# The first query's projection takes its PSUM bank from the retention's pool instead of the shared projection pool

## The chip, the cores and the metric

The kernel runs on one core of a Trainium2 chip. The metric is the device time of one execution, in microseconds. Engines are named as in the profile: PE (TensorE, matrix multiplies), PEld (its weight loads), DVE (VectorE), ACT (ScalarE), POOL (GpSimd) and SP (SyncE, which only issues DMAs here).

## The reference

Two layers of a hybrid transformer on one sequence of 512 tokens, model width 1024, followed by a final norm. Each layer computes

```
h      = rms_norm(x)
proj   = h @ w_in                       # retention | DSA | dilated columns
mixed  = concat(retention_mixer, dsa_mixer, dilated_mixer)
x      = x + mixed @ w_out
x      = x + square(relu(rms_norm(x) @ w_up)) @ w_down
```

The retention mixer has 4 heads. The DSA mixer has 4 heads which attend to 128 selected keys per query (an indexer scores all keys, and a top-k picks them). The dilated mixer has 8 heads with three window patterns, which the kernel folds into one mask. All heads are 64 wide.

## The kernel before

Everything is kept in fp32 and multiplied as a high and a low part, so each projection of 128 columns (`wform`) is 8 blocks x 3 products = 24 matmuls of 128x512 into one PSUM bank. PSUM has 8 banks, in three pools: `mm` with two banks (all projections), `at` with four (scores, transposes, attention outputs), `rt` with two. The `rt` pool serves the four retention tiles of a layer (`ret_tile`), tokens 2 and 3 of the dilated values (`dil_v`: tokens 0 and 1 take `mm`, tokens 2 and 3 take `rt_bank()`) and a part of the MLP's down projection.

The attention part of a layer is emitted in this order: stage `tv` (token columns), `idx` (the indexer), `top` (the first round of the top-k), `dv0` (first half of the dilated values); then the projections of the first head pair, `q_of(heads[0], ...)` and `k_of(heads[0], ...)` (called q0 and k0 below); then a loop over 12 heads, in which `head_s` issues the scores and the softmax of a head, and the list `FILL` (`'q1,q2 k1 k2,g0,d g1,k3,...'`) adds the next projections: q1 beside head 0, then q2, k1 and k2, and so on. The `topk` rounds (16 per layer, each three MAX8 and three match-and-replace steps on DVE, lines 603 and 604) are spread over the same loop.

A projection that has ended in its bank is taken out of it in two halves of 64 partitions. `evac_q` (lines 424 and 425) does for each half an ACT activation and then a DVE operation which subtracts what ACT has written. `evac_k` (lines 437 to 439) does the same with a copy, a DMA of the high part and a DVE subtraction. The bank is free for the next projection when the second DVE operation has ended.

The Tile framework orders the instructions of each engine when the program is built: by their place in the code, shifted by the hand-set numbers in `PR`, and by its own model of when operands, buffers and banks come free. At run time each engine works through its queue in that fixed order. A bank is given to a tile by the same planner, out of those free in its pool at that point of the plan.

Weights come by DMA into `raw`, are split by ACT (line 278) and POOL or DVE (line 286) into one of 5 `w` buffers, and `done()` prepares the next unit after a projection has used one.

Of the kernel before, what the change touches and what calls it, by code (L numbers as in the profile page):

```python
# [123 lines left out]
class Kern:  # L124
# [665 lines left out]
        return self.evac_k(ps)  # L790

    def proj(self, key, act, cols=P):
        ps = self.mm()
        self.wform(self.unit(key), act, cols, ps, cols)
        self.done()
        return ps
# [336 lines left out]
```

## Time and profile before

| | |
|---|---|
| Median of 3 runs | 1234.67 us (1234.22 to 1235.9) |
| The profiled execution, device time | 1234.49 us |
| Its span, first to last instruction | 1232.7 us |
| PE busy | 1209.2 us, 98% of the span |
| DVE busy | 922.2 us, 75% |
| ACT busy | 678.8 us, 55% |
| POOL busy | 476.2 us, 39% |

The profiled execution lies 0.18 us below the median of the runs, and its time is 1.8 us above its own span. Busy times are sums over the whole program, which has stages with different limits: attention and MLP of layer 0, then the same for layer 1, whose first projection starts at 622 us.

### The profile page before, as it was taken

Reading aid. Unit: us, or ns where it says so; the run is one execution under the profiler, and the core shown is the slowest. Engines: PE = TensorE matmul, PEld = TensorE weight load, DVE = VectorE, ACT = ScalarE, POOL = GpSimd, SP = SyncE. Lnnn points to the kernel's source line nnn. Section 1 sums busy time; section 2 is a strip of 40 time slices with the busy share of each in tenths; the row PEclk is TensorE's granted clock in tenths of the full one; section 3 lists DMA queues with packets and bytes.
Section 4 is the critical chain, followed back from the end, with each engine's and each line's share of the span. In section 5 each row is a group of like instructions: output and inputs, shape, how many; then the busy total and the mean of one; then the engine's idle time right before and its main releaser. Section 6 shows DMA issues by size and latency. Waiting matters only on the chain. (4 is left out here: it accounts for less than half of the span.)

```text
span 1232.7 us, 16897 instructions
## 1 busy us (share of the span) xinstructions
PE 1209.2 (98%) x6116; PEld 1028.4 (83%) x6116; DVE 922.2 (75%) x1582; ACT 678.8 (55%) x1241; POOL 476.2 (39%) x461
## 2 busy tenths in 40 slices
PE   8999999999999999999999999999999999999997
PEld 6988888889888888888889888888798888888886
DVE  5599858776875967858857997687769668587596
ACT  6645658745544545545556456686455355354454
POOL 4443747553402304114223546764544032140232
PEclk9999999999999999999999999999999999999999
DMA  7432314216244071260153323241180622604201
GB/s 217 120 94 65 103 56 124 82 52 210 64 145 129 2 220 52 74 179 16 46 163 95 95 79 93 86 120 52 52 257 1 208 65 69 180 26 142 81 1 69
DMA packets 142180, 122.73 MB, mean 100 GB/s; under 512 B 6801, under 2 KB 114065, under 8 KB 142098
## 3 DMA queue, kind: packets, MB, share of 16 engines
q1 hardware_dynamic: 139600, 117.46, 31.9%
q10 hardware_dynamic: 2498, 4.20, 1.3%
q8 instruction: 48, 0.79, 0.3%
q14 instruction: 34, 0.28, 0.1%
HBM read 114.31 MB, written 4.19 MB: 96 GB/s over the span
## 5 line engine op out<-in xcount | busy, mean ns | idle before, releaser
L336 PE MATMUL mm<-act,w 128*128 128x512 f32 (+2 forms) x2352 | 516.1, 377 | 3.1 <-DVE Q L425 3.1
L336 PEld LDWEIGHTS mm<-act,w 128*128 128x128 f32 x2352 | 424.4, 188 | 79.8 <-issue 3.9
L286 POOL TENSOR_TENSOR w<-raw,w 128x512 fp32r<-128x512 f32 (+1 forms) x124 | 160.5, 1318 | 98.0 <-ACT w L278 73.0
L278 ACT CAST w<-raw 128x1024 fp32r<-128x1024 f32 (+1 forms) x138 | 143.1, 1038 | 77.3 <-PE rt L1039 27.6
L1039 PE MATMUL rt<-w,U 128*128 128x512 f32 x768 | 183.2, 389 | 0.0
L286 DVE TENSOR_TENSOR w<-rd,w 128x1024 fp32r<-128x1024 f32 x112 | 144.8, 1305 | 49.9 <-ACT w L278 49.9
L286 DVE TENSOR_TENSOR w<-raw,w 128x1024 fp32r<-128x1024 f32 (+1 forms) x76 | 93.8, 1235 | 102.0 <-ACT w L278 101.8
L1039 PEld LDWEIGHTS rt<-w,U 128*128 128x128 f32 x768 | 144.2, 188 | 29.9
L996 POOL TENSOR_TENSOR st<-s 128x256 f32<-128x256 f32 x32 | 39.1, 1222 | 330.1 <-ACT s L985 325.2
L278 ACT CAST w<-rd 128x1024 fp32r<-128x1024 f32 x112 | 117.5, 1049 | 83.4 <-PE rt L1039 41.7
L348 PE MATMUL mm<-w,act 128*128 128x456 f32 (+2 forms) x576 | 119.4, 353 | 2.2 <-DVE KL L439 1.2
L348 PEld LDWEIGHTS mm<-w,act 128*128 128x128 f32 x576 | 96.8, 190 | 15.3 <-DVE act L401 1.6
L348 PE MATMUL mm<-w,mix 128*128 128x512 f32 x384 | 98.3, 404 | 0.6 <-DVE Q L425 0.5
L1039 PE MATMUL at<-w,U 128*128 128x512 f32 (+1 forms) x396 | 97.7, 386 | 0.0
L304 DVE TENSOR_TENSOR rd<-rd,rd 128x1024 f32<-128x1024 f32 x64 | 94.3, 1473 | 0.6
L1039 PEld LDWEIGHTS at<-w,U 128*128 128x128 f32 x396 | 73.6, 188 | 15.0
L348 PEld LDWEIGHTS mm<-w,mix 128*128 128x128 f32 x384 | 71.2, 192 | 15.3 <-DVE Q L425 0.9
L983 ACT ACTIVATE s<-mm 128x512 f32<-128x512 f32 x62 | 36.9, 595 | 85.2 <-PE mm L336 75.6
L1000 ACT CAST U<-st 128x1024 fp32r<-128x1024 f32 x32 | 33.8, 1055 | 81.0 <-POOL st L997 81.0
L994 POOL TENSOR_TENSOR st<-s,s 128x256 f32<-128x256 f32 x32 | 36.7, 1146 | 92.0 <-ACT s L985 92.0
L464 ACT ACTIVATE ph<-ph,sm 128x128 f32<-128x128 f32 (+1 forms) x96 | 53.9, 563 | 24.6 <-DVE sm L463 23.6
L1001 DVE TENSOR_TENSOR U<-s,U 128x256 fp32r<-128x256 f32 x64 | 63.9, 999 | 0.0
(169 smaller groups left out, 1770.8 us busy)
## 6 DMA issues: line engine op xcount, KB each, us to landing
raw<-in_w_up_dram SPq DMA_DIRECT2D x64, 512.0 KB, 4.3
rd<-in_w_down_dram SPq DMA_DIRECT2D x32, 1024.0 KB, 5.1
raw<-in_w_in_dram SPq DMA_DIRECT2D x48, 512.0 KB, 3.9
raw<-in_w_out_dram SPq DMA_DIRECT2D x16, 512.0 KB, 4.1
xv<-in_x_dram SPq DMA_DIRECT2D x7, 512.0 KB, 4.8
KH<-KH ACTq DMA_DIRECT2D x24, 128.0 KB, 2.3
raw<-in_w_in_dram SPq DMA_DIRECT2D x8, 256.0 KB, 2.9
xd<-xv SPq DMA_DIRECT2D x4, 512.0 KB, 2.8
```

The source lines that it names most:

```text
L278: self.nc.scalar.copy(hi, src)
L286: eng.tensor_tensor(lo[:, i:i + step], src[:, i:i + step], hi[:, i:i + step].bitcast(F32), op=ALU.subtract)
L304: sub = lambda o, a, b: self.nc.vector.tensor_tensor(o, a, b, op=ALU.subtract)
L336: self.nc.tensor.matmul(ps[:cols, toks[0]:toks[1]], a, b, start=(k == 0 and j == 0), stop=(k == KB - 1 and j == 2))
L348: self.nc.tensor.matmul(ps[:, :w], a, b, start=(n == 0), stop=(n == tot - 1))
L464: nc.scalar.activation(p, p, AF.Exp, bias=a, scale=-1.0, accum_out=b)
L983: nc.scalar.activation(s, ps, AF.Relu)
L994: tt(st[:, 0], a[:, 1], d[:, 1], op=ALU.add)
L996: tt(st[:, 2], a[:, 0], a[:, 1], op=ALU.subtract)
L1000: nc.scalar.copy(hi, src)
L1001: nc.vector.tensor_tensor(lo, src, hi.bitcast(F32), op=ALU.subtract)
L1039: nc.tensor.matmul(ps[:, c0:c1], a, w, start=(new and n == 0), stop=(n == 11), skip_group_check=True)
```

## The change

`proj` makes the bank of a projection and is called by `q_of`, `k_of` and `gate`. For the key whose second and third items are `"dq"` and `0` (the dilated query projection of head pair 0, once in each layer), the tile now comes from `rt_bank()`; all other projections still call `mm()`. The number and form of the instructions are the same; the bank of q0, and what follows from it in the planner's order, is what can differ.

```
     def proj(self, key, act, cols=P):
-        ps = self.mm()
+
+        ps = self.rt_bank() if key[1:3] == ("dq", 0) else self.mm()
         self.wform(self.unit(key), act, cols, ps, cols)
         self.done()
         return ps
```

## Rows read from the trace of the kernel before

**Rows 1.** The cores view: span and mean granted TensorE clock.
```profile
core 0: 1232.7 us, clock 0.995
```

**Rows 2.** The page, part 1: busy us, share of the span, instructions.
```profile
PE 1209.2 (98%) x6116; PEld 1028.4 (83%) x6116; DVE 922.2 (75%) x1582; ACT 678.8 (55%) x1241; POOL 476.2 (39%) x461
```

**Rows 3.** Waits of PE, whole program: who waited for whom, total us, times, longest.
```profile
PE mm L336 <- DVE Q L425: 3.1, 2, 1.6
PE mm L348 <- DVE KL L439: 1.2, 2, 0.6
```

**Rows 4.** Timeline of layer 0, 72 to 92 us: start, us, engine, line, operation.
```profile
72.67 11.07 PE L336 MATMUL mm<-act,w 128*128 128x512 f32 x48
72.69 0.39 ACT L525 CAST xv<-rt 128x256 fp32r<-128x256 f32 x1
...
77.19 1.47 DVE L603 MAX8 top<-sc 128x8 f32<-128x384 f32 x3
78.34 0.59 ACT L424 ACTIVATE Q<-mm 64x512 fp32r<-64x512 f32 x1 [3.76 <-PE mm L336]
...
80.15 1.47 DVE L603 MAX8 top<-sc 128x8 f32<-128x384 f32 x3
81.65 0.68 DVE L425 SCALAR_TENSOR_TENSOR Q<-mm,Q 64x512 fp32r<-64x512 f32 x1
82.37 0.59 ACT L424 ACTIVATE Q<-mm 64x512 fp32r<-64x512 f32 x1 [2.50 <-DVE Q L425]
...
84.48 0.69 DVE L425 SCALAR_TENSOR_TENSOR Q<-mm,Q 64x512 fp32r<-64x512 f32 x1
...
85.32 5.73 PE L336 MATMUL mm<-act,w 128*128 128x512 f32 x24 [1.58 <-DVE Q L425]
85.45 0.53 ACTq L438 DMA_DIRECT2D KH<-KH  x1
...
88.30 0.69 DVE L439 TENSOR_TENSOR KL<-mm,KH 64x512 fp32r<-64x512 f32 x1
...
90.88 0.22 PE L444 MATMUL at<-KH,Q 128*128 128x128 f32 x1
...
91.12 0.70 DVE L439 TENSOR_TENSOR KL<-mm,KH 64x512 fp32r<-64x512 f32 x1
```

**Rows 5.** Timeline of PE in layer 0, after those rows.
```profile
92.16 4.72 PE L336 MATMUL mm<-act,w 128*128 128x512 f32 x20
...
97.30 0.40 PE L348 MATMUL rt<-w,act 128*128 128x256 f32 x2
...
127.37 3.10 PE L348 MATMUL mm<-w,act 128*128 128x256 f32 x24 [0.60 <-DVE KL L439]
```

**Rows 6.** Timeline of DVE in layer 0 just before 127.37 us.
```profile
126.53 0.69 DVE L439 TENSOR_TENSOR KL<-mm,KH 64x512 fp32r<-64x512 f32 x1
```

**Rows 7.** Busy time by stretch: length, then PE, PEld, DVE, ACT, POOL busy (instructions), clock, DMA.
```profile
72.67:127.37 54.70, 52.29 (x272) 44.00 (x270) 53.94 (x162) 29.48 (x60) 24.85 (x26) 1.00 0.33 84
...
142.00:190.00 48.00, 47.69 (x255) 40.36 (x253) 26.94 (x79) 29.77 (x66) 28.59 (x32) 1.00 0.28 81
679.88:734.55 54.67, 52.29 (x271) 44.00 (x270) 53.91 (x162) 29.47 (x60) 24.85 (x26) 1.00 0.32 84
```

**Rows 8.** DVE groups from 72.67 to 127.3 us: count, busy us, mean ns.
```profile
L604 DVE MATCH_REPLACE8 sc<-top,sc 128x512 f32<-128x512 f32 (+2 forms) x36 | 19.6, 550 | 0.1
L603 DVE MAX8 top<-sc 128x8 f32<-128x384 f32 (+2 forms) x36 | 18.6, 546 | 0.1
```

**Rows 9.** Timeline of layer 1, the same place as rows 4.
```profile
692.51 5.69 PE L336 MATMUL mm<-act,w 128*128 128x512 f32 x24 [1.56 <-DVE Q L425]
...
698.32 0.69 DVE L439 TENSOR_TENSOR KL<-mm,KH 64x512 fp32r<-64x512 f32 x1
...
699.31 4.76 PE L336 MATMUL mm<-act,w 128*128 128x512 f32 x20
```

**Rows 10.** The page, part 6: DMA of the key's high part, us to landing.
```profile
KH<-KH ACTq DMA_DIRECT2D x24, 128.0 KB, 2.3
```

More of the change, by code (lines that the diff above doesn't have):

```diff
@@ L792, in proj @@
     def proj(self, key, act, cols=P):
-        ps = self.mm()
+        ps = self.rt_bank() if key[1:3] == ("dq", 0) else self.mm()
         self.wform(self.unit(key), act, cols, ps, cols)
```

## The prediction

> **What bounds the kernel now.** I read the cores view first: one core, span 1232.7 us, TensorE at a mean granted clock of 0.995 [rows 1], which is the upper of its two levels (2.4 GHz) nearly throughout; nothing here hangs on the clock. The page's first part comes next: TensorE is busy for 98% of the span, VectorE for 75% [rows 2]. So over the whole program TensorE is the bound, and time can be won only where TensorE idles, or by less work for it; the change takes no work away.
>
> The third view is therefore TensorE's waits. The reader is to see one entry: TensorE's projections (line 336) wait for VectorE's line 425 twice, 3.1 us together, the longest 1.6 [rows 3]. This is the largest wait inside the layers, and 0.25% of the time. The timeline shows what it is. In layer 0 the 48 matmuls of q0 and k0 run from 72.67 to 83.74, into the two `mm` banks. The next projection, q1, needs one of these banks. That of q0 is free when the second half of `evac_q` ends on VectorE, at 84.48 + 0.69 = 85.17, and q1 starts 0.15 us later, at 85.32, after 1.58 us of idleness [rows 4]. Layer 1 does the same, with 1.56 us [rows 9].
>
> The change aims at exactly this wait. Whether it pays depends on the view read last, the busy time by stretch. From 72.67 to 127.37 us VectorE is busy for 53.94 of 54.70 us, and in layer 1 for 53.91 of 54.67 [rows 7]. The remainder, 0.76 us in each, is spread over 162 instructions. In this stretch it is VectorE that has no slack, whatever the 75% of the page say: 36 MAX8 and 36 match-and-replace steps of the top-k, 18.6 + 19.6 us, are queued between the evacuations [rows 8]. The first evacuation shows how late it runs: ACT ends the first half of q0 at 78.34 + 0.59 = 78.93, and VectorE's part starts at 81.65, behind rank work, 2.72 us later [rows 4].
>
> **The change part by part.** *The wait for q0's bank goes.* With q0 in a retention bank, k0 and q1 have the two `mm` banks, and q1 can start when k0 ends, at 83.74 instead of 85.32: 1.58 us in layer 0 and 1.56 in layer 1, 3.14 together [rows 4, 9].
>
> *What is late next.* q1 takes 90.88 - 85.32 = 5.56 us up to the scores of head 0, and these take 92.16 - 90.88 = 1.28 us [rows 4, 5]. Moved up, q1 ends at 89.30 and the scores at 90.58. The scores' own operands allow that: the first half of k0's low part is ready at 88.30 + 0.69 = 88.99, and the DMA issued at 85.45 lands some 2.3 us later, about 87.8 [rows 4, 10]. Behind the scores stands q2, and it needs an `mm` bank too. Of these, q1's has only just been filled; k0's is free when VectorE has done k0's second half, at 91.12 + 0.70 = 91.82 [rows 4]. With the 0.15 us seen above q2 starts at 91.97. It starts at 92.16 now [rows 5]. So of the 1.58 us, 0.19 remain, and TensorE waits 91.97 - 90.58 = 1.39 us at q2 instead, for line 439 instead of 425. In layer 1 the same bank is free at 698.32 + 0.69 = 699.01, q2 could start at 699.16, and starts at 699.31 now: 0.15 remain [rows 9]. Queued behind q2 on TensorE is everything else of the layer, since its queue is in order; no other matmul can fill the 1.39 us unless the planner has put one there.
>
> *And after that.* The 0.19 and 0.15 us do not reach the end either. At 127.37 TensorE waits again for VectorE, 0.60 us, for the low part that ends at 126.53 + 0.69 = 127.22 [rows 5, 6]. VectorE comes to this point through 54.55 us of nearly unbroken work, and none of this work becomes shorter or starts earlier by an earlier matmul. As long as VectorE's queue keeps its order, TensorE is at 127.37 when it was before. The remainder goes there, and the term of this part is 0 (bounds from this part: 0 to -0.34 us).
>
> *The retention bank as such.* The two `rt` banks hold tokens 2 and 3 of the dilated values until ACT has read them, for the first at 72.69 + 0.39 = 73.08, which is 0.41 us after q0's start of before [rows 4]. Either the planner lets k0 begin and switches to q0 when its bank is free, and TensorE loses nothing; or TensorE stands until 73.08 + 0.15 = 73.23, 0.56 us. Then k0 ends at 84.30, q1 at 89.86 and the scores at 91.14, still ahead of 91.97: the late bank is hidden by the wait at q2, and its term is 0. Without that cover it costs 2 x 0.56 = 1.12 us. At its other end the bank is held until 85.17, and the next matmuls into an `rt` bank start at 97.30 [rows 4, 5]: 12 us of room, term 0.
>
> *What follows q1's earlier end on other queues.* The number of instructions and DMAs is unchanged. ACT's evacuation of q1 and the split of the weights that take q1's buffer can come some 1.6 us earlier; ACT is busy for 29.48 of 54.70 us here and POOL for 24.85 [rows 7], neither sets the end, so 0.
>
> The sum for the profiled execution is 1234.49 - 0 = 1234.5 us. It lies 0.18 us under the median of the runs, and I put the forecast between the two: **1234.6 us**, no change. About 0.2% (2.5 us) is what a measurement of this kernel can tell from no change.
>
> **The rivals.** *First, the full gain: about 1231.4 us.* The orders of the queues are planned when the program is built. If the planner, with a bank more, puts the evacuations further ahead and rank work behind 127.37 us, the wait does not come back at q2, and 1234.49 - 3.14 = 1231.4. For it: 38.2 us of the stretch are rank work, which no matmul near it waits for, and from 142 to 190 us VectorE is busy for 26.94 of 48.00 us only [rows 7, 8], so there is room to put it. Against it: the plan must move more than 1.25 us of rank work per layer past TensorE's wait at 127.37 us, and the change touches no priority. The evacuation started 2.72 us after its operand was there [rows 4], which says that the plan had VectorE further ahead than it is; in the plan q0's bank was then free well before k0's end at 83.74, and a planner that sees no wait changes nothing by its removal. The bound of this case is all idleness of TensorE in the two stretches, (54.70 - 52.29) + (54.67 - 52.29) = 4.8 us [rows 7], thus 1229.7.
>
> The Trainium skill (Perfetto Trace Analysis, section Matmuls) asks that independent matmul groups rotate through different PSUM banks, so that the evacuation of one overlaps the matmuls of the next. By that rule alone the time would be this rival's, 1231.4 us; the trace agrees that the bank is what q1 waits for (1.58 us), and speaks against the rest of it, as the rotation meets the next late bank 1.28 us further on.
>
> *Second, slower: about 1237.4 us.* The retention bank is free 0.41 us later than q0's bank was needed; the planner then puts q0 a little later, or k0 first, and VectorE's queue is filled differently from there on: what stands before an evacuation is rank work in pieces. One set of three MAX8, 1.47 us [rows 4], put ahead of the evacuations before 127.37 in each layer makes TensorE later there by 1.47 us twice: 1234.49 + 2.94 = 1237.4. It decides from 1.25 us per layer on. For it: VectorE is full up to 127.22, so each piece put ahead is paid in full. Against it: the shift is small beside the 2.72 us by which VectorE lags, and the plan of layer 1 repeats that of layer 0 closely although much else differs (busy 53.91 against 53.94 us by 162 instructions each [rows 7]).
>
> *Third, the bank comes late and this is not hidden: 1234.49 + 1.12 = 1235.6 us.* It needs both a strict order of q0 before k0 and an evacuation of k0 that ends earlier than now. It is within the 0.2%.
>
> That the change does nothing at all can be excluded for the bank itself, as its key is met once in each layer; for the order it is part of the forecast.
>
> **How the numbers follow.** Forecast 0.48, third rival 0.08, full gain 0.24, slower 0.20. Within 0.2% lie the forecast and the third: 0.56. Faster by more than 0.2% is the first: 0.24, slower by more the second: 0.20. The likeliest case by itself spans 1233.8 to 1235.9, from the 0.34 us of the remainder to the highest run shown. The range has to hold 8 in 10, so it takes in the values of both outer rivals with a little beyond each, but not their bounds: 1230.9 to 1237.6.
>
> **What would show it.** In the profile of the changed kernel: the 48 matmuls of q0 and k0 with one half written to `rt`, q1 directly behind them, and no wait for line 425 there. Right behind the scores of head 0, q2 with a wait of about 1.4 us for line 439. VectorE with as many rank steps as now before 127.4 us, and TensorE's wait there grown from 0.60 to about 0.8. The forecast is wrong if VectorE shows fewer than 36 of each rank step before the low part that ends at 127.22 now (then the first rival), or more (then the second), or if something other than q2 follows the scores.

## The result and the profile after

The changed kernel takes 1250.32 us (median of 4 runs, 1246.56 to 1253.69) against 1234.63 us of the kernel before on the same chip: a ratio of 1.0126, with a 95% interval of 1.0111 to 1.0142. It is slower by 15.6 us, six times what a measurement can tell, and far above the range given. (A loss that stands with a ratio is taken from that ratio, an estimate from all runs of one job; the difference of the two medians can deviate from it by up to 2 us.) The profiled execution is the fastest of the four, 1246.56 us. Lines below `proj` are numbered one higher than before (1040 for 1039).

The cores view and the first part of the page after answer to [rows 1, 2]. The span grew by 12.1 us; TensorE is busy 7.2 us longer by the same 6116 matmuls, and idle 4.9 us longer.

```profile
core 0: 1244.8 us, clock 0.993
```
```profile
PE 1216.4 (98%) x6116; PEld 1032.8 (83%) x6116; DVE 922.5 (74%) x1582; ACT 678.2 (54%) x1241; POOL 475.3 (38%) x461
```

TensorE's waits after, beside [rows 3]. The wait for line 425 at line 336 is gone, as the change meant. In its place stands a wait of the scores (line 444) for a DMA, and at the end of the attention the waits for transposed probabilities (line 486) have grown.

```profile
PE at L444 <- DMA KH<-KH: 5.0, 3, 3.5
PE at L492 <- ACT PT L486: 2.2, 4, 0.8
```

The timeline of layer 0 after answers to [rows 4]:

```profile
72.68 4.95 PE L336 MATMUL mm<-act,w 128*128 128x512 f32 x21
72.70 0.40 ACT L525 CAST xv<-rt 128x256 fp32r<-128x256 f32 x1
77.47 5.60 PE L336 MATMUL rt<-act,w 128*128 128x512 f32 x24
82.91 6.28 PE L336 MATMUL mm<-act,w 128*128 128x512 f32 x27
83.11 0.59 ACT L424 ACTIVATE Q<-rt 64x512 fp32r<-64x512 f32 x1 [8.52 <-PE rt L336]
91.82 0.30 PE L444 MATMUL at<-KH,Q 128*128 128x128 f32 x1 [1.35 <-DMA KH<-KH]
```

TensorE begins with 21 matmuls of k0 and then does the 24 of q0, in `rt`; the last 3 of k0 and the 24 of q1 follow without a wait. The first `rt` bank was free at 72.70 + 0.40 = 73.10, but q0 starts at 77.47. The order was fixed when the program was built, so I take it that the planner had counted on the bank later; its model was not looked into. So q0's first evacuation starts at 83.11, not at 78.34. And what follows the scores of head 0 is no longer q2: the scores of head 1 come first, at 91.82. They use the second half of the key, whose high part must cross over by DMA, and wait 1.35 us for it.

To see where the 12.1 us are I cut both layers at three marks that exist in both traces: the first matmul of q0 or k0; the matmul of line 779 that waits for line 624; the first ACT operation of the MLP (line 983, after: 984). The stretch from the first to the second is called the top-k stage below, that from the second to the third the tail. Columns as in [rows 7]. Before:

```profile
72.67:186.52 113.85, 111.14 (x591) 94.83 (x590) 92.82 (x280) 65.14 (x140) 61.30 (x66) 1.00 0.31 85
186.52:302.62 116.10, 113.36 (x673) 97.78 (x674) 86.93 (x211) 71.40 (x165) 63.96 (x70) 0.99 0.34 103
679.88:793.72 113.84, 111.15 (x591) 94.85 (x590) 92.79 (x280) 65.12 (x140) 61.31 (x66) 1.00 0.31 85
793.72:910.06 116.34, 113.50 (x673) 97.81 (x674) 87.51 (x211) 70.73 (x166) 64.35 (x70) 0.99 0.34 103
```

After:

```profile
72.68:186.30 113.62, 111.50 (x591) 94.89 (x590) 94.90 (x279) 64.29 (x140) 60.83 (x66) 1.00 0.31 85
186.30:305.37 119.07, 114.05 (x673) 96.96 (x674) 84.73 (x211) 71.60 (x167) 64.03 (x70) 1.00 0.33 101
682.62:800.76 118.14, 113.96 (x592) 97.29 (x590) 94.36 (x279) 64.65 (x140) 61.07 (x66) 0.97 0.29 82
800.76:922.14 121.38, 116.59 (x673) 99.48 (x674) 86.68 (x211) 71.65 (x166) 64.01 (x70) 0.97 0.33 98
```

The four differences are -0.23, +2.97, +4.30 and +5.04 us, together 12.08: all of it. The first one lies within the 0.34 us that I had left for the remainder, but not by the steps that I had forecast: what follows the scores of head 0 there is not q2. The loss sits in layer 1's top-k stage and in both tails. The tails begin more than 100 us behind the changed projection, and have the same 673 matmuls.

In layer 1's top-k stage the timeline shows the same wait as in layer 0, but longer:

```profile
699.79 0.37 SPq L263 DMA_DIRECT2D raw<-in_w_in_dram  x1
700.08 0.47 ACTq L438 DMA_DIRECT2D KH<-KH  x1
704.69 0.45 PE L444 MATMUL at<-KH,Q 128*128 128x128 f32 x1 [3.53 <-DMA KH<-KH]
```

The key's DMA, issued at 700.08, 0.3 us behind a load of weights, lands 4.5 us later; the two of the first key in this layer before took 2.2 to 2.3 us. In layer 0 the same DMA was issued at 88.99, ahead of that load (89.84), and landed 2.7 us later. What made the difference stands at the very start of the two stages, where one and the same operation of VectorE took 0.28 us in layer 0 and 1.43 us in layer 1. VectorE has no slack here, and carried the 1.15 us along to the evacuation of the key:

```profile
72.88 0.28 DVE L594 SCALAR_TENSOR_TENSOR sc<-masks,sc 128x128 f32<-128x128 f32 x1
682.82 1.43 DVE L594 SCALAR_TENSOR_TENSOR sc<-masks,sc 128x128 f32<-128x128 f32 x1
```

In the kernel before this operation took 1.42 us in both layers. So the -0.23 us of layer 0 compare a stage with the short one to a stage with the long one; that the number comes near my forecast is luck.

After 3.53 us without a matmul TensorE then gets half its clock. Stretches of 2 us, with the granted clock and the DMA share in the third and second columns from the end:

```profile
702.00:704.00 2.00, 0.00 (x0) 0.00 (x0) 1.91 (x6) 0.17 (x2) 1.75 (x2) 1.00 0.91 267
704.00:706.00 2.00, 1.31 (x6) 1.34 (x6) 1.93 (x8) 1.98 (x7) 0.74 (x1) 0.55 0.14 22
706.00:708.00 2.00, 2.00 (x6) 1.64 (x6) 2.00 (x10) 1.11 (x4) 0.00 (x0) 0.50 0.89 241
708.00:710.00 2.00, 2.00 (x6) 1.59 (x5) 1.94 (x8) 1.53 (x5) 0.93 (x2) 0.50 0.04 12
710.00:712.00 2.00, 2.00 (x8) 1.54 (x8) 1.52 (x7) 0.72 (x1) 0.93 (x2) 0.74 0.00 0
```

Busy time at a clock below full costs (1 - clock) x busy: 0.45 x 1.31 + 0.50 x 4.00 + 0.26 x 2.00 = 3.1 us. I use this sum below as "the clock's loss" of a stretch. With it the stage's +4.30 is +1.49 of idle time (118.14 - 113.96 against 113.84 - 111.15) and +2.81 of busy time, which the clock's loss accounts for.

The tail of layer 0 before, on TensorE:

```profile
242.98 0.32 PE L674 MATMUL rt<-rT 64*128 64x128 f32 x1
...
255.34 3.11 PE L348 MATMUL mm<-w,mix 128*128 128x512 f32 x13
...
261.50 0.97 PE L492 MATMUL at<-PT,vs 128*128 128x384 f32 x6
...
264.00 0.32 PE L674 MATMUL rt<-rT 64*128 64x128 f32 x1 [0.67 <-ACT rT L665]
```

The same place after:

```profile
245.98 0.32 PE L674 MATMUL rt<-rT 64*128 64x128 f32 x1
...
259.47 0.38 PE L492 MATMUL at<-PT,vs 128*128 128x256 f32 x1 [0.82 <-ACT PT L486]
260.09 2.35 PE L348 MATMUL mm<-w,mix 128*128 128x512 f32 x9 [0.24 <-DVE xv L832]
...
263.97 0.44 PE L492 MATMUL at<-PT,vs 128*128 128x384 f32 x1 [0.28 <-ACT PT L486]
264.85 1.30 PE L492 MATMUL at<-PT,vs 128*128 128x384 f32 x5 [0.45 <-DVE PT L487]
```

Before, 13 matmuls of the output projection (line 348 on `mix`) stand at 255.34, and the attention outputs (line 492) then run without a wait. After, four more waits have come in, 1.79 us. The third retention tile (line 674), which began at 242.98 before, begins at 245.98, and matmuls of the output projection have been done in its place. The order of the tail has changed, not its work.

### The profile page after: what moved, and what is told of

Read it like the earlier page. It is cut to its first block, busy times and chain, and to the rows that moved or that the text cites. A ratio compares the mean times of both kernels' runs of the same rounds, so it can differ in the third digit from the quotient of the medians.

```text
span 1244.8 us, 16882 instructions
## 1 busy us (share of the span) xinstructions
PE 1216.4 (98%) x6116; PEld 1032.8 (83%) x6116; DVE 922.5 (74%) x1582; ACT 678.2 (54%) x1241; POOL 475.3 (38%) x461
## 5 line engine op out<-in xcount | busy, mean ns | idle before, releaser
L336 PE MATMUL mm<-act,w 128*128 128x512 f32 (+2 forms) x2304 | 506.6, 378 | 0.2 <-DVE P L646 0.2
L336 PEld LDWEIGHTS mm<-act,w 128*128 128x128 f32 x2304 | 417.3, 189 | 74.9 <-DVE P L646 0.5
```

The source lines that it names most:

```text
L336: self.nc.tensor.matmul(ps[:cols, toks[0]:toks[1]], a, b, start=(k == 0 and j == 0), stop=(k == KB - 1 and j == 2))
```

## The experiments

Two causes are thus proposed: the **start** (q0 within k0, head 1's scores ahead of q2, waiting for the key's DMA), and the **tail** (another planned order). Rivals: that the tail is late because the start is; that q0's bank in itself loses time; that the full gain of a removed wait is to be had otherwise. Stage lengths are compared with those of before above. "Old" and "new" tail mean the place of the third retention tile in the planned order: as in the kernel before, or 14 matmuls later, as after. Where the view names another operation for the wait of head 1's first scores (e3, e9, e14), it is still the key's DMA: in all ten such waits of 1.2 to 4.0 us the matmul starts 0.13 to 0.14 us after the DMA has landed.

**e1_q0_at** keeps q0 out of the projections' banks, but in a bank that is free in time.

```
-        ps = self.rt_bank() if key[1:3] == ("dq", 0) else self.mm()
+        ps = self.at() if key[1:3] == ("dq", 0) else self.mm()
```

> q0's projection takes its bank from the pool of four (scores, transposes) instead of the retention's. These banks are free when q0 begins, so the planner keeps q0, k0, q1 in the order of before and only the bank differs. Order theory (the loss comes from the retention bank being planned free only 21 matmuls into k0, so that q0 is put behind it and the whole layer is planned anew): no wait of TensorE for line 425 at 83.7 us, a wait of about 1.4 us for line 439 at q2, TensorE at 127.4 us as before, and a time near that of before, 1233 to 1238 us, as only small later shifts of the plan remain. Any-change theory (each change of the plan of this kernel costs about as much): 1245 us or more. Full-gain theory: 1231.4 us.

Measured: 1243.33 us against 1235.47, ratio 1.0071 (1.0056 to 1.0086), +8.8 us (7.9 by the medians), a time that none of the three theories had. TensorE in layer 0 and layer 1:

```profile
91.87 4.34 PE L336 MATMUL mm<-act,w 128*128 128x512 f32 x18 [1.49 <-DVE KL L439]
...
701.85 4.35 PE L336 MATMUL mm<-act,w 128*128 128x512 f32 x18 [1.50 <-DVE KL L439]
```

The start keeps its order, and the wait comes back at q2, 1.49 and 1.50 us; I had worked out 1.39. The top-k stages are 113.70 and 113.66 us, 0.15 and 0.18 shorter than before (the operation of line 594 is the long one in both kernels). But both tails have the new order:

```profile
186.28:305.29 119.01, 113.92 (x673) 96.95 (x674) 84.76 (x211) 71.62 (x165) 64.04 (x70) 1.00 0.33 100
...
796.21:919.06 122.85, 118.05 (x673) 100.76 (x674) 86.74 (x211) 71.66 (x165) 64.13 (x70) 0.96 0.32 97
```

So the tail's loss needs neither the retention bank nor a late start.

**e2_rt_layer0** and **e3_rt_layer1** make the change in one layer only.

```
-        ps = self.rt_bank() if key[1:3] == ("dq", 0) else self.mm()
+        ps = self.rt_bank() if key[:3] == (0, "dq", 0) else self.mm()    # e3: (1, "dq", 0)
```

> The retention bank for q0 in layer 0 alone. Order theory, from the profile of the changed kernel: layer 0 is 2.8 us longer there, layer 1 9.3 us, so 1237.4 us here, and layer 1 shows the 1.56 us wait of before. If the waits for the key's DMA depend on when it lands, 1236 to 1241. If the two layers' losses are linked (layer 1 is slow because layer 0 ends elsewhere), the sum of this run's loss and that of the run with layer 1 alone is not that of both.

> The retention bank for q0 in layer 1 alone. Order theory: layer 0 as before, and in layer 1 the wait for the DMA of the key's high part (3.5 us, then some microseconds of half clock) and the later order: 1241 to 1246 us. If layer 1's loss is only an accident of when its weights are loaded after a longer layer 0, about 1237.5 us as with layer 0 alone.

Measured: 1244.0 us, ratio 1.0069 (1.0047 to 1.009), and 1240.92, ratio 1.005 (1.0035 to 1.0065). Their losses, 8.5 and 6.2 us, add up to 14.7, close to the 15.6 of both; e2 is slower than I had expected, because its layer 0 has the long wait that layer 0 of the changed kernel was spared. In e2 layer 0 is longer by 3.93 (top-k stage, wait for the key's DMA 3.70 us) and 5.54 (tail), and layer 1 as before; in e3 layer 1 is longer by 2.74 (wait 3.40) and 3.88, and layer 0 is not. The loss is local to the layer that has the edit.

**e4_k0_first_mm** issues k0 ahead of q0, both in the projections' banks.

```
-        q_of(heads[0], (L, "dq", 0, 0))
         k_of(heads[0], (L, "dk", 0, 0))
+        q_of(heads[0], (L, "dq", 0, 0))
```

> k0's projection is emitted ahead of q0's, both in the projection pool's two banks as before; no retention bank. Theory that the late q0 (its evacuation crowding that of k0) is what costs: slower than before by 3 us or more, with the scores of head 0 waiting for the key's DMA or for q0's low part. Theory that the later order of the layer (240 to 300 us) costs and not the start: within 1233 to 1237 us.

Measured: 1235.17 us, ratio 1.0001 (0.9989 to 1.0012). The trace has more to tell than the time:

```profile
82.00 0.47 ACTq L438 DMA_DIRECT2D KH<-KH  x1
```
```profile
91.12 0.22 PE L444 MATMUL at<-KH,Q 128*128 128x128 f32 x1
```

Here too q0 stands behind k0 and the first of head 1's scores come ahead of q2, at 91.12, and these scores do not wait: all of k0 is done first, and its second DMA is issued at 82.00. In the changed kernel k0 is split, 21 matmuls ahead of q0 and 3 behind it, so this DMA is issued at 88.99, nearly as late as before (89.63), while the scores that need it have moved up. So neither q0 behind k0 nor that order of the scores costs, nor both together; they cost where k0 is split, so that the key comes late.

**e5_rt_tail, e6_at_tail, e7_before_tail** alter one priority, to move the tail back: in the changed kernel, in e1's, and in the kernel before.

```
-    'PR': {... 'hs_9': 400, ...
+    'PR': {... 'hs_9': 300, ...
```

> The changed kernel with one hand-set priority altered (head 9: 300 instead of 400), which lets the plan put the third retention tile about 2.3 us of TensorE work earlier, near its place in the kernel before; the start of the attention (q0 within k0, head 1's scores ahead of q2) is that of the changed kernel. Theory: two separate losses, the wait for the key's DMA at the start and the late retention tile at the tail, about 7 us and 8 us. Then this one shows the first alone: 1242 us (1240 to 1244), the waits of 1.35 and 3.5 us at line 444 still there and no pile of waits at 259 to 272 us. Rival, the tail's waits are a consequence of the late start and not of the plan: 1248 to 1250 us with the waits still there. Second rival, the start costs nothing by itself: 1235 us.

> q0's bank from the scores' pool instead of the retention's, and the same priority of head 9 (300): the start's order is that of the kernel before and the tail's plan close to it. The change's own mechanism alone. My forecast's mechanism: the wait of 1.58 us comes back as 1.5 us at q2, the time is that of the kernel before with the same priority, 1235 us (1233.5 to 1236.5). Theory of the late retention tile: the same number, as the 8 us of e1_q0_at go with the tile. Rival, e1's loss came from the bank taken out of the scores' pool or from the start: 1243 us again.

> Control: the kernel before with the same priority of head 9 (300). If the priority by itself neither wins nor loses, 1235 us (1233.5 to 1236.5), and e5 and e6 can be read against it. If it wins or loses by more than 2 us, e5 and e6 are to be read as differences to this run.

Measured: 1245.3, 1238.16 and 1235.3 us (ratios 1.0078, 1.003, 1.0012; the last from 0.9997 to 1.0026). All but the control lie above what I had expected. The control's time is fair (its own tail order is not quite the old one), but the test is not what I meant it to be: the priority gives e5 and e6 a third order of the tail, neither old nor new, with 4.3 and 4.4 us of idle time in e6. Against its control e6 loses 2.9 us, its tails being 117.56 and 117.39 us and its top-k stages 113.68 and 113.69. e5 has the DMA's wait in both layers, 4.00 and 3.68 us, its top-k stages 3.12 and 3.00 longer.

**e8_no_key_dma** takes the DMA out of the changed kernel for the first key of each layer.

```
             nc.scalar.copy(kh[r, s, :], ps[r, :])
-            nc.scalar.dma_start(kh[o, s, :].bitcast(F32), kh[r, s, :].bitcast(F32))
+            if self.nkl == 1:
+                nc.scalar.copy(kh[o, s, :], ps[r, :])
+            else:
+                nc.scalar.dma_start(kh[o, s, :].bitcast(F32), kh[r, s, :].bitcast(F32))
```

> The changed kernel in which the first key's high part is brought to the other 64 partitions by a copy of ACT out of the PSUM bank, not by a DMA (two copies of about 0.6 us for two DMAs per layer; the other keys as before). TensorE's order at the start stays that of the changed kernel, with head 1's scores ahead of q2; the plan of the tail goes back to that of the kernel before by itself. Theory: both losses gone, 1235 us (1232 to 1237), TensorE waiting at most 0.5 us at line 444 near 92 and 704 us, and no half clock from 704 to 710 us. Rival, what costs at the start is the order itself (q2 behind head 1's scores, q0 behind 21 matmuls of k0) and not the DMA: 1240 to 1243 us.

Measured: 1237.72 us, ratio 1.0028 (1.0017 to 1.0038), a little above what I had expected: most of the loss is gone, but not all. The plan went back to the old tail (115.61 us in layer 0), and no matmul waits for the DMA. At the start TensorE now waits for the next things that are late, the key's low part and a split of weights (lines below the edit are three higher):

```profile
90.25 0.33 PE L448 MATMUL at<-KL,Q 128*128 128x128 f32 x1 [0.55 <-DVE KL L442]
...
93.01 0.80 PE L348 MATMUL rt<-w,act 128*128 128x256 f32 x2 [1.23 <-ACT w L278]
```

The top-k stages are longer by 2.57 and 1.44 us, with a clock's loss of 3.26 and 1.66. ACT, with two copies more, is what is late at 93.01. So the rival holds in part, as far as the two added copies are not the cause themselves: with head 1's scores ahead of q2, TensorE has no work in front of things that are only just being made, and the DMA is the latest of them.

**e9_rt_oldtail, e10_at_oldtail, e11_before_k1** are the same three kernels with another priority.

```
-    'PR': {... 'fill_k1': 20, ...
+    'PR': {... 'fill_k1': 0, ...
```

> The changed kernel with one priority altered by 20 (fill_k1 0 instead of 20). The start of the attention stays that of the changed kernel (q0 behind 21 matmuls of k0, head 1's scores ahead of q2, the key's DMA), the retention tiles of the tail come in the plan where the kernel before has them. Theory of two losses: the tail's piled waits are gone (idle time of TensorE from the end of the top-k stage to the MLP 2.7 to 3.2 us a layer, not 5.0), the wait for the key's DMA stays: 1240 us (1238 to 1243). Rival, the tail is late because the start is: 1248 us or more. Rival, the start costs nothing: 1235 us.

> q0's bank from the scores' pool, and the same priority (fill_k1 0). Start in the order of the kernel before, tail with the retention tiles where the kernel before has them. Only the removed wait is left of the change. My forecast's mechanism: the wait comes back as 1.5 us at q2, and the time is that of the kernel before, 1234.5 us (1233 to 1236), where e6, whose retention tiles 1 and 2 are placed differently, was 3.8 us slower. Rival, the full gain of a removed wait: 1231.4 us. Rival, q0 in another pool is a loss by itself: 1238 us or more.

> Control for the two others: the kernel before with the same priority (fill_k1 0). Theory: the plan of start and tail stays, 1234.5 us (1233 to 1236); what it differs by from the kernel before is to be taken off e9 and e10.

Measured: 1238.72, 1242.47 and 1235.29 us (1.0043, 1.0075, 1.0018). e9 is 3.4 us above its control; its tails have 2.7 and 3.0 us of idle time, as before, and its loss is layer 1's top-k stage, 4.45 us longer than before with a wait of 3.71 us at head 1's scores (layer 0's tail is 1.64 longer by the clock, whose loss there is 3.4 us and was 1.6). e10 contradicted my expectation. Its trace shows why: layer 0 has the old tail (its 119.31 us hold 5.0 of the clock's loss), but in layer 1 the order flipped again, with a longer top-k stage and 5.1 us of idle time in the tail. A priority shift of 20 was not enough to hold both.

**e12_k0_at** gives the spare bank to k0, so that neither q1 nor q2 meets a late one.

```
-        ps = self.rt_bank() if key[1:3] == ("dq", 0) else self.mm()
+        ps = self.at() if key[1:3] == ("dk", 0) else self.mm()
```

> The key's projection k0, and not q0, takes a bank of the scores' pool; q0 and q1 have the two projection banks, and q2's bank is q0's, free early. So neither q1 nor q2 waits for a bank, and the tail's plan is that of the kernel before. My step that VectorE alone sets 127.4 us: no wait at q1 or q2, TensorE's wait near 127.4 us grown by about 1.5 us or spread over the heads before it, time unchanged, 1234.5 us (1233 to 1236). Rival, the full gain: 1231.4 us, with the point of 127.4 us at about 125.8. Theory of the key's DMA: if head 0's or head 1's scores come right behind their key, TensorE waits 1 to 4 us at line 444 instead and the time is 1237 us or more.

Measured: 1234.3 us against 1233.25, ratio 1.0012 (0.9999 to 1.0026). TensorE waits at no bank near the start. It waits at the low part of the key further on, 1.14 us where it was 0.60 [rows 5], and then for another operation of VectorE. That first wait ends 52.05 us after the stage's first matmul, where it was 54.70, so VectorE's order has changed too:

```profile
123.97 3.10 PE L348 MATMUL mm<-w,act 128*128 128x256 f32 x24 [1.14 <-DVE KL L439]
...
129.59 2.65 PE L348 MATMUL mm<-w,act 128*128 128x256 f32 x20 [0.53 <-DVE P L646]
```

The top-k stages are 0.84 and 0.83 us shorter than before, but that can't be put down to the removed waits: the operation of line 594 is the short one in both layers here. In e4, e13 and e15, which have one of each, the stage with the short one is shorter by 1.2 to 1.7 us. Nothing measurable arrives in the time.

**e13_at_oldtail2, e14_rt_oldtail2, e15_before_q2** are again e1, the changed kernel and the one before, with a priority that keeps the old tail in both layers. **e16_q1_rt** gives the retention bank to q1, a start without the key's wait; its plan has the old tail in layer 0 and the new one in layer 1.

```
-    'PR': {... 'fill_q2': 20, ...
+    'PR': {... 'fill_q2': 50, ...
```
```
-        ps = self.rt_bank() if key[1:3] == ("dq", 0) else self.mm()
+        ps = self.rt_bank() if key[1:3] == ("dq", 1) else self.mm()      # e16
```

> q0's bank from the scores' pool and one priority altered by 30 (fill_q2 50 instead of 20): start in the order of the kernel before, and in the plan the retention tiles of both layers where the kernel before has them (e10 had that in layer 0 only). My forecast's mechanism alone. If the tail's plan caused the loss of e1_q0_at: 1234.5 us (1233 to 1236.5), top-k stages 113.7 us as in e1, tails with 2.7 to 3.0 us of idle time and not 5. If q0 in another pool loses time by itself: 1238 us or more.

> The changed kernel with the same priority (fill_q2 50): its own start with the key's DMA, tails planned as in the kernel before in both layers. The start's loss alone: 1239 us (1237 to 1241), as e9_rt_oldtail (1238.7), with the wait of 3.5 to 4 us at line 444 in at least one layer. If the start is harmless: 1235 us.

> Control for e13 and e14: the kernel before with the same priority (fill_q2 50), plan of start and tail kept: 1234.5 us (1232.5 to 1236). What it differs by from the kernel before is to be taken off e13 and e14.

> q1, and not q0, takes a retention bank: another start, in which neither q1 nor head 0's scores wait for an evacuation. In the plan the tail of layer 0 is that of the kernel before, the tail of layer 1 that of the changed kernel. If the tail's plan decides: layer 1's tail 2.5 to 6 us longer than layer 0's and than the 116.3 us of before, idle time there 5 us against 2.7 to 3, in all 1237 to 1240 us. If the tail's loss comes from q0's bank: both tails as before, 1232 to 1235 us.

Measured: 1235.06, 1241.05, 1235.54 and 1240.09 us (1.0016, 1.0069, 1.0004, 1.005). The stages of e13:

```profile
73.39:186.58 113.19, 111.48 (x592) 94.93 (x590) 93.91 (x280) 65.25 (x140) 61.11 (x66) 1.00 0.31 85
186.58:302.17 115.59, 112.36 (x673) 96.60 (x674) 87.47 (x211) 70.88 (x165) 64.10 (x70) 1.00 0.33 103
679.43:794.35 114.92, 111.64 (x592) 94.91 (x590) 94.62 (x280) 65.33 (x140) 61.04 (x66) 1.00 0.30 84
794.35:909.43 115.08, 112.13 (x673) 96.67 (x674) 86.86 (x211) 71.28 (x166) 63.74 (x70) 1.00 0.34 105
```

Those of its control e15:

```profile
72.02:185.22 113.20, 111.49 (x591) 94.98 (x590) 93.91 (x280) 65.34 (x140) 61.12 (x66) 1.00 0.30 85
185.22:300.70 115.48, 112.19 (x673) 96.63 (x674) 87.49 (x211) 70.88 (x165) 64.10 (x70) 1.00 0.34 104
677.97:792.88 114.91, 111.54 (x592) 94.84 (x590) 94.61 (x280) 65.32 (x140) 61.06 (x66) 1.00 0.30 84
792.88:908.04 115.16, 112.22 (x673) 96.66 (x674) 86.86 (x211) 71.27 (x165) 63.74 (x70) 1.00 0.34 105
```

The top-k stages agree to 0.01 us, although in e15 q1 waits 0.43 and 1.57 us for line 425 and in e13 it does not; there q2 waits 0.35 and 1.50 us for line 439 instead. (In both runs the operation of line 594 is short in layer 0 and long in layer 1.) With the order held, moving q0's bank neither wins nor loses anything that these runs could tell: by the medians e13 is 0.5 us faster than e15, by the ratios it is slower by 0.12%, and each ratio's interval reaches 0.12% to either side. In e14 the start alone costs 5.5 us over the control by the medians; in its trace the long wait is in layer 0:

```profile
94.90 0.45 PE L444 MATMUL at<-KH,Q 128*128 128x128 f32 x1 [3.93 <-DVE sm L463]
```

(The view names an operation of line 463; the key's DMA, an operand of this matmul, was issued at 90.14 and landed 4.6 us later, 0.14 us ahead of 94.90.) And e16, without q0's bank and without the key's wait, has the tail's loss in the one layer whose plan has it:

```profile
185.85:301.33 115.48, 112.40 (x673) 96.61 (x674) 87.54 (x211) 70.81 (x165) 64.28 (x70) 1.00 0.34 104
...
792.31:915.16 122.85, 118.10 (x673) 100.73 (x674) 86.76 (x211) 71.75 (x167) 64.07 (x70) 0.96 0.32 96
```

Of tails at full clock throughout, the old order took 115.1 to 115.6 us (ten of them, in e3, e8, e9, e11, e12 and e16, and both of e13 and e15) and the new one 119.0 (layer 0 of after and of e1). So the order is worth 3.4 to 4.0 us a layer, before any loss of clock. Half of it is not idle time: layer 0 of after has 1.8 us more idle and 1.7 us more busy time than layer 0 of e13, for the same 673 matmuls in another order.

## Why the prediction was wrong

**The mechanism forecast was right where the order holds, and was not what decided.** That q1's wait goes, that it returns at q2 for line 439, and that nothing measurable reaches the end: e1 shows the first two (1.49 and 1.50 us), e13 beside e15 the third. In the changed kernel itself q1's wait goes, but q2 does not follow, and the forecast's own sign of being wrong came true. The Trainium skill's rule of rotating banks (Perfetto Trace Analysis, section Matmuls) describes what e12 does in full; the trace agrees that the waits go, and shows no gain in time.

**The step that failed first is "The retention bank as such".** It offered two ways: the planner lets k0 begin and switches to q0 when its bank is free, "and TensorE loses nothing", or TensorE stands for 0.56 us. The first happened, and it loses. I had dated the switch by the trace, 0.41 us after the start; the planner, which goes by its own model, put q0 21 matmuls into k0, 4.8 us late. The end of k0 stays behind q0, so the key is as late as before, while the plan has head 1's scores ahead of q2. What is on the path then is the key's DMA. In layer 0 its wait of 1.35 us is hidden as the wait at q2 would have been: TensorE is at 127.32 where I had forecast 127.37. Waits of 3.4 to 4.0 us are not, and the half clock behind them costs 1.5 to 3.2 us more. The prediction had the DMA's 2.3 us and no more; it had asked whether head 0's scores have their operands, and not what a changed order would put there. The DMA took 4.5 us in layer 1. This term measured 3.4 us (e9 over e11) to 5.5 (e14 over e15) by the medians, in place of 0.

**The second failure is an omission: that nothing behind 127.37 can move.** "A planner that sees no wait changes nothing by its removal" is what I took for it. The planner saw a different bank, moved a few instructions, and more than 100 us later two retention tiles and the output projection came in another order. That is the larger part: 8.8 us in e1, where it stands alone, and none in e13, where it is taken away. That the tail's loss follows the plan and not q0's bank, e16 shows.

**A reading failed too: "nothing here hangs on the clock".** The tails of the kernel before hold 1.6 and 1.7 us of the clock's loss; after, layer 1 holds 3.1 in its top-k stage and 3.4 in its tail, and layer 0 none. About 3 of the 12.1 us are the clock's.

**The rivals.** The second (slower) had the sign and the thought that the plan may be refilled, but looked for it on VectorE's queue ahead of 127.37 and priced it at 2.9 us. Before that low part VectorE did 37 of each rank step in layer 0, against 36 [rows 8], but the low part ends at 127.26, as late as before (127.22), so no loss came of it there. The full gain did not come in any variant, and the third's 0.56 us did not occur.

**What stays open.** The tail measured 8.8 us by its ratio (7.9 by medians), the start 3.1 to 8.0 by ratios (3.4 to 5.5 by medians). Together that is 11.3 to 16.8, around the 15.6 (13.7 to 17.5) measured, and e2 and e3 make 14.7. Whether the two losses strengthen each other through the clock, these runs don't settle. Why the planner's order in the tail flips was not followed step by step in the planner. The new tail was never made in the kernel before without moving a bank.

No version beat the kernel before: of those that move a bank, e12 and e13 come nearest, with ratios of 1.0012 and 1.0016.

## What to carry to other kernels

Where a framework orders the queues by its own model, an edit of one buffer is also an edit of the plan: before costing the wait that goes, list what else the new order could bring forward, and which DMA or evacuation its operands would need. A change whose own mechanism is worth nothing can still cost 1% by a flipped order far behind it; a second variant with the same mechanism and the old order (here a priority moved by 30) separates the two. A wait for a bank that is followed by the next late thing of the same engine is worth little: find the point up to which that engine is full. And before reading a difference of a microsecond between two traces as the edit's, see whether the same operations took the same time in both.

## What the runs showed of the hardware

One operation of VectorE had two lengths. The operation of line 594 (597 in e8) that starts 0.2 us after the first matmul of a top-k stage, and 0.02 us behind one of GpSimd (line 286), took 0.27 to 0.28 us in 12 of the 36 stages and 1.42 to 1.43 us in the other 24; GpSimd's took 1.45 to 1.46 us beside the short one and 1.29 to 1.30 beside the long one. Five kernels had one of each in their two layers with the same order at the start (after, e9, e13, e14, e15). Wherever TensorE has the order of before, q1 waits 1.56 to 1.58 us with the long one and 0.42 to 0.43 with the short one (e11, and layer 0 of e15); so some 1.15 us of the wait that the change aimed at came from this operation. Why it has two lengths, the runs don't show.

The same tail order takes different times in different executions. In layer 0 of before, e3, e4, e9, e10, e11 and e14 TensorE's 673 matmuls come in the same order. With equal waits ahead of it (0.68 and 0.53 us at line 674), the clock's loss of that tail was 0 (e3, e11), 1.6 (before), 3.4 (e9) or 5.0 us (e4 and e10); the granted clock in these stretches goes to 0.50, the lower level of 1.2 GHz. The 29 runs of before in one job spread from 1229.78 to 1237.3 us. In or right after a wait of 3.4 to 4.0 us at the start the clock fell each time (e2, e3, e5 twice, e9, e14, after); after the single waits of 1.2 to 1.4 us there it did not (after, e9, e14). The Trainium skill (TensorE: Matmul & The Clock Gate, section What's actually happening) says that the hardware's check of activity runs free of the kernel; the spread of equal waits agrees with it.

The key's DMA of 128 KB took 2.2 to 2.3 us from issue to landing for the first key of the kernel before, and 4.3 to 4.7 us in the seven waits of 3.4 to 4.0 us, where a load of weights had been issued on SP's queue 0.3 us ahead of it. Where the next load was issued 0.8 to 0.9 us behind it, it took 2.5 to 2.7 us (layer 0 of after and e9, layer 1 of e14). Over all traces, the 38 DMAs of a key that were issued at most 0.4 us behind a load took 4.0 to 5.5 us; the median of those with no load in the 2 us ahead is 2.2 us. In layer 1 of after, the DMA queues show where the time went: in the 2.6 us from 700.1 to 702.7 only SP's queue (q1) moved packets, and all 80 packets of the key's (q10) came in the 1.9 us from 702.7 on, beside 324 more of q1 (packets, MB, share of 16 engines; the lines are from these two windows):

```profile
q1 hardware_dynamic: 847, 0.48, 72.9%
...
q10 hardware_dynamic: 80, 0.13, 25.4%
```

The Trainium skill (DMA: Bandwidth & Descriptors, section Queues, rings and completion order) has each DMA engine take turns between the queues that it has work for, packet by packet. The trace shows packets of both queues from 702.8 to 703.4, but none of the key's ahead of that. With no load beside it, the same DMA of the kernel before moved its first packet at 86.6, 1.2 us after its issue at 85.45; here the first came 2.7 us after the issue. Why it came so late, the runs don't show.
